# A hybrid decoder trunk on one core: scores read negated and scaled, an undivided first softmax, roots' rows by the values' bank, and a cast tied later

## The chip, the core and the metric

One core of one Trainium2 chip runs the whole program. Its engines are TensorE (PE; PEld is its weight load), VectorE (DVE), ScalarE (ACT), GpSimd (POOL) and SyncE (SP, which only issues transfers here). The metric is the device time of one execution in microseconds; the time of a kernel is the median of its runs.

## The reference

One layer works on 512 tokens of 1024 features. After a modulated RMS norm, one projection feeds two token mixers. Mixer A is a sliding-window attention (window 128, 8 query heads on 2 key heads, a sink for each head). Mixer B is a differential attention with 4 heads. Cut to what the change touches:

```python
# A: per head, with a sink as one more column of the softmax
bias = -slopes[:, :, None, None] * delta
scores = where(valid, scores + bias, -1e30)
probs = softmax(concatenate([scores, sink], -1), -1)[..., :-1]
# B: two maps per head, their difference, a norm over the head's 128 values
scores = scores - slopes * delta            # causal
p = softmax(scores, -1)
a = p[:, :, 0] - lam * p[:, :, 1]
out = einsum('bhqs,bshe->bqhe', a, v)
out = out * rsqrt(mean(out * out, -1) + 1e-6) * subln_g * (1 - lam_init)
```

Both mixers go through a branch projection and a sigmoid gate, are added, and go through an output projection (`merged @ w_out`); then follow a norm, a gated MLP of 2816 features with a short causal convolution, and a final norm.

## The kernel before

Every product runs in three passes: an operand is split into a high part (a cast on ScalarE, e.g. line 118) and a low part (a subtraction on VectorE), and `mm3` (lines 120 to 123) multiplies high by high, high by low and low by high. PSUM's eight banks are handed out under four names: f (2, for projections), s (3, scores), t (2, transposes) and v (1, values). An instruction that writes a bank waits until the bank's last tenant was read.

The order of TensorE's work is written by hand (`manual_schedule`). The projections are generators that give one `mm3` a step; `fill(n)` (line 519) takes n such steps ("ticks") between two pieces of an attention, so that TensorE has projections to multiply while the other engines do the softmax. `after(n, fn)` runs `fn` n ticks later. VectorE's and ScalarE's order in the attentions comes from priorities: what stands under `high_priority` is placed as soon as its operands can be there, and `issue_after` ties an instruction behind another. Each engine takes its own list in order.

Mixer A runs in four pairs of heads (j = 0, 1). `swa_scores` multiplies queries (`qa`) and keys into an s bank and one VectorE operation adds the distances and takes the greatest score (line 582); `swa_softmax` turns the greatest into the negated shift `nm` (593), has ScalarE take exponentials with their sums (597) and divides (605). The first pair begins while VectorE still empties the banks of the opening projections: `keep_v` (455) splits the values' banks `av0` to `av3` into `vvh` and `vvl`, and `stack` (431) makes `qa[:, 1]` for the second pair.

Mixer B runs in four heads of four blocks of queries (n = 0 to 3, with (n+1) x 128 keys). `diff_scores` and `diff_softmax` do the same for two maps; the two sums are inverted together, the second is multiplied by -lambda (`nlam`), the second map is scaled (704) and the first is scaled and added (705). `diff_transpose` turns the result on TensorE (`td`) and splits it into `aTh` and `aTl`; `diff_values` (720) multiplies it with the values into the v bank (`od`). Six ticks behind, `stats` sums squares on TensorE (`pss`, a t bank), a root follows on VectorE and GpSimd, `to_rows` (99) turns the root's column on TensorE (a t bank again), ScalarE copies it out (103), and two transfers spread it as a row `rb`; `spread` multiplies the head by `rb` and splits it (`vv`). `double` (443) makes the doubled keys `qk` of a head, the last two copies of 64 x 1024 on ScalarE (450).

Behind the mixers, `load_rows` loads the eight row blocks of the output weight (`wo`), each scaled by the first gate and split. `to_rows` also turns the second gate's column (`g2`, line 983), the last use of a t bank ahead of the output projection, whose eight accumulators (`oc`) take all eight banks. `prep(0, "m5", ...)` (1135) splits `m5w`, the sum of two blocks of the MLP's weight, which an accumulating transfer of GpSimd puts together (1076). Where these splits stand on ScalarE and VectorE follows from priorities and ties alone.

Of the kernel before, what the change touches and what calls it, by code (L numbers as in the profile page):

```python
# [8 lines left out]
F32 = mybir.dt.float32  # L9
# [22 lines left out]
G1_AT = 12  # L32
STAT_LAG = 6
ROW_LAG = 6
NORM_LAG = 20
# [11 lines left out]
def kernel(  # L47
# [45 lines left out]
    def vbank(name):  # L93
        return bank("v", 1, [P, S], name)
# [4 lines left out]
    def to_rows(dst, lo, n, name):  # L99
        turned = tbank(name, (P, P))  # L100
        nc.tensor.transpose(turned, cols[:, lo + n - P : lo + n], ident)
        part = cpool.tile([32, P], F32, tag="part", name=name + "p")
        nc.scalar.copy(part, turned[96:])
        d = dp.tile([n, P], F32, name=name + "d")
        nc.gpsimd.dma_start(d, part[32 - n :])
        nc.gpsimd.dma_start(dst, d.rearrange("k q -> (k q)").partition_broadcast(P))
# [336 lines left out]
    def double(dst, src):  # L443
        with tc.high_priority(offset=HP):
# [4 lines left out]
            for j, (own, other) in enumerate(halves):  # L449
                nc.scalar.copy(dst[other, j], dst[own, j])  # L450
# [109 lines left out]
    def swa_scores(i, n0):  # L560
        if n0 == 0:
            c = pairs[i] = Pair()
            c.mx, c.nm, c.lsum, c.es = (
                ap.tile([P, 2, NT], F32, tag=t, bufs=2, name=f"{t}{i}") for t in ("mx", "nm", "lsum", "es")
# [13 lines left out]
        for j in range(2):  # L578
            for n in (n0, n0 + 1):
                w = P if n == 0 else 2 * P  # L580
                with tc.high_priority(offset=HP):
                    c.last = nc.vector.tensor_tensor_reduce(
                        c.sb[n][:, j, :w], sps[j][:, n - n0, :w], dsw[:, 256 - w : 256], 1.0, -3e38, ALU.add, ALU.max,
                        c.mx[:, j, n : n + 1],
                    )

    def swa_softmax(i):
        with tc.high_priority(offset=HP):
            c = pairs[i]
            for j in range(2):  # L590
                h = i + 4 * j
                slope = 2.0 ** -(h + 1)
                nc.vector.tensor_scalar(c.nm[:, j], c.mx[:, j], -slope, nsink[:, h : h + 1], ALU.mult, ALU.min)
                nc.scalar.activation(c.es[:, j], c.nm[:, j], AF.Exp, bias=sink[:, h : h + 1])
                for n in range(NT):
                    w = P if n == 0 else 2 * P
                    nc.scalar.activation(
                        c.sb[n][:, j, :w], c.sb[n][:, j, :w], AF.Exp, bias=c.nm[:, j, n : n + 1], scale=slope,
# [64 lines left out]
    def diff_scores(*ss):  # L663
# [14 lines left out]
        for s, sps, w in ops:  # L678
# [3 lines left out]
            for m in range(2):  # L682
                st = ap.tile([P, w], F32, tag="st", bufs=ST, name=f"sd{h}_{n}_{m}")
                with tc.high_priority(offset=HP):
                    nc.vector.tensor_tensor_reduce(
                        st, sps[m], ddf[:, 512 - w : 512], 1.0, -3e38, ALU.add, ALU.max, mx[:, m : m + 1]
# [4 lines left out]
    def diff_softmax(s):  # L691
        with tc.high_priority(offset=HP):
            h, n = divmod(s, NT)
            slope = 2.0 ** (-2 * (h + 1))
            mx, pm = scored[s]
            lsum = ap.tile([P, 2], F32, tag="dls", bufs=3, name=f"dls{h}_{n}")
            nc.vector.tensor_scalar_mul(mx, mx, -slope)  # L697
            for m in range(2):
                nc.scalar.activation(  # L699
                    pm[m], pm[m], AF.Exp, bias=mx[:, m : m + 1], scale=slope, accum_out=lsum[:, m : m + 1]  # L700
                )
            nc.vector.reciprocal(lsum, lsum)
            nc.vector.tensor_mul(lsum[:, 1:2], lsum[:, 1:2], nlam)
            nc.vector.tensor_scalar_mul(pm[1], pm[1], lsum[:, 1:2])
            end = nc.vector.scalar_tensor_tensor(pm[0], pm[0], lsum[:, 0:1], pm[1], ALU.mult, ALU.add)
# [14 lines left out]
    def diff_values(h):  # L720
# [14 lines left out]
        def stats():  # L735
            pss = tbank(f"pss{h}", (P, NT))
# [3 lines left out]
            rstd_m2(rs, pss, NT, P, ap)  # L740
# [9 lines left out]

            after(ROW_LAG, lambda: to_rows(rb, NCOL + NT * h, NT, f"rs{h}"))
            after(NORM_LAG, spread)

# [51 lines left out]
    pairs, firsts, scored, probs, aTs = {}, {}, {}, {}, {}  # L805
# [12 lines left out]
    with tc.issue_after(pairs[0].last.ins), tc.issue_after(vat_copy.ins):  # L818
        with tc.high_priority(offset=HP):
            keep_v(6, (1,))  # L820
        swa_softmax(0)
        stack(qa[:, 1], acc[2], qsc[:, 1:2], soon=False, high=False)
        keep_v(4, (1,))
# [43 lines left out]
    for s in range(4 * DIFF_HEADS):  # L867
# [19 lines left out]
        if n == 0 and h:  # L887
            diff_values(h - 1)
            fill(DIFF_FILL[3])
# [143 lines left out]
    wo = []  # L1033
    for k in range(KT):
        with ExitStack() as place:
            for b in recent if k == 0 else merged[-2:] if k == 6 else ():
                place.enter_context(tc.issue_after(b.ins))
            wo.append(load_rows(wout, k, f"wo{k}", g1b))

# [95 lines left out]
    prep(0, "m5", (m5w[:, 0], m5w[:, 1]))  # L1135
# [711 lines left out]
```

## Time and profile before

| | |
|---|---|
| median of three runs | 680.46 us (680.43 to 682.62) |
| the profiled execution | 680.85 us, span 679.1 us |
| granted TensorE clock, mean | 0.998 |

Each row of a timeline gives a start, a duration, the engine, the line, the operation with output and inputs (partitions x elements), and in brackets how long the engine sat idle before it and what released it. "x2" stands for so many instructions in a row. TensorE's matmuls overlap: those of 128 x 512 last 0.39 us each and start every 0.227 us. A row of waits names who waited, for what, the total in us, how often, and the longest. Times in the text are from the start of the span.

### The profile page before, as it was taken

To read this page: it belongs to the slowest core of one execution; us is meant where nothing else is said; L and a number is where in the kernel's file an instruction comes from. 1 tells how busy PE (TensorE), PEld (TensorE's weight loads), DVE (VectorE), ACT (ScalarE), POOL (GpSimd) and SP (SyncE) were. 2 spreads that over 40 slices of the span, in tenths; PEclk is the share of its full clock that TensorE was granted. 3 is DMA by queue.
4 is the path that set the end of the run, shared out by engine and by line. 5 is a ranking of instruction groups with operands and counts; after the bars stand their busy time and mean duration, and the time that the engine had idled before them with its cause. 6 is when DMAs were issued, how large, how long until landed. Compare 5 with 4: busy or idle time off the path is not lost.

```text
span 679.1 us, 10811 instructions
## 1 busy us (share of the span) xinstructions
PE 666.5 (98%) x4021; PEld 591.7 (87%) x4021; DVE 569.8 (84%) x1055; ACT 402.6 (59%) x704; POOL 71.8 (11%) x86
## 2 busy tenths in 40 slices
PE   8999999999999999989999999999999999999995
PEld 8888888788888888868899999999999998888885
DVE  6988887779887678953689998888888999979997
ACT  6678879455655323232597656565556566656665
POOL 2000000000001000010020110011111003440300
PEclk9999999999999999999999999999999999999999
DMA  8961132444365698567374988887976658996903
GB/s 351 409 240 66 63 100 88 136 144 149 91 195 171 215 322 265 196 204 245 117 125 110 222 212 202 195 201 167 216 173 181 144 186 196 194 200 191 165 0 124
DMA packets 71876, 121.78 MB, mean 179 GB/s; under 512 B 4208, under 2 KB 48016, under 8 KB 71824
## 3 DMA queue, kind: packets, MB, share of 16 engines
q1 hardware_dynamic: 52960, 95.04, 41.6%
q0 software_dynamic: 18576, 25.71, 22.4%
q8 instruction: 31, 0.51, 0.3%
q10 hardware_dynamic: 288, 0.34, 0.2%
q14 instruction: 21, 0.17, 0.1%
HBM read 118.97 MB, written 2.11 MB: 178 GB/s over the span
## 4 chain that ended last, share of the span: by engine, by line
PE 82%; DVE 8%; DMA 5%; ACT 3%; issue 1%; POOL 0%; SPq 0%; ACTq 0%; POOLq 0%
PE up L1173 33%; PE dc L1776 15%; PE av L364 3%; DMA s_t<-in_w_up_dram 2%; PE oc L1229 2%; PE oc L1233 2%; PE oc L1230 2%; DMA wbd<-in_w_branch_diff_dram 2%; PE pga L121 2%; PE pga L122 2%; DVE ra L772 2%; PE aqa L361 2%; PE pga L123 2%; PE sw L577 1%; PE sd L674 1%
## 5 line engine op out<-in xcount | busy, mean ns | idle before, releaser
L1173 PE MATMUL up<-t,m_whi 128*128 128x256 f32 x512 | 93.1, 283 | 0.0
L1173 PEld LDWEIGHTS up<-t,m_whi 128*128 128x128 f32 x512 | 79.9, 192 | 0.0
L1173 PE MATMUL up<-t,m_wlo 128*128 128x256 f32 x256 | 72.4, 283 | 0.0
L1173 PE MATMUL up<-bh,p_whi 128*128 128x256 f32 x232 | 65.7, 283 | 0.0
L1173 PE MATMUL up<-bl,p_whi 128*128 128x256 f32 x232 | 65.7, 283 | 0.0
L1173 PE MATMUL up<-bh,p_wlo 128*128 128x256 f32 x232 | 65.7, 283 | 0.0
L1173 PEld LDWEIGHTS up<-t,m_wlo 128*128 128x128 f32 x256 | 49.2, 192 | 0.0
L1173 PEld LDWEIGHTS up<-bh,p_whi 128*128 128x128 f32 x232 | 44.5, 192 | 0.0
L1173 PEld LDWEIGHTS up<-bl,p_whi 128*128 128x128 f32 x232 | 44.5, 192 | 0.0
L1173 PEld LDWEIGHTS up<-bh,p_wlo 128*128 128x128 f32 x232 | 44.5, 192 | 0.0
L1076 POOL DMA_DIRECT2D s<-in_w_up_dram x21 | 27.0, 1366 | 157.5 <-DMA s<-in_w_up_dram 102.3
L1104 ACT CAST m_whi<-s 128x1024 fp32r<-128x1024 f32 x31 | 32.5, 1048 | 15.7 <-DVE s L1098 9.1
L772 DVE CUSTOM_DVE_ANT_0 ra<-ra,csb 128x1024 f32<-128x1024 f32 x32 | 38.6, 1219 | 2.8 <-DMA ra<-in_w_ada_t_dram 2.8
L1108 DVE TENSOR_TENSOR m_wlo<-s,m_whi 128x1024 fp32r<-128x1024 f32 x31 | 37.7, 1217 | 1.3 <-ACT m_whi L1104 1.3
L1173 PE MATMUL up<-t,p_whi 128*128 128x256 f32 x176 | 32.2, 283 | 0.0
L1173 PEld LDWEIGHTS up<-t,p_whi 128*128 128x128 f32 x176 | 27.4, 192 | 0.1
L699 ACT ACTIVATE sd<-sd,dmx 128x128 f32<-128x128 f32 (+3 forms) x32 | 17.8, 557 | 16.3 <-DVE dmx L697 12.1
L1104 ACT CAST p_whi<-wa 128x1024 fp32r<-128x1024 f32 x18 | 18.8, 1043 | 12.6 <-PE up L1173 5.4
L1180 ACT ACTIVATE gT<-a,cols 128x512 f32<-128x512 f32 x22 | 17.6, 813 | 13.4 <-DVE a L1215 13.0
L1108 DVE TENSOR_TENSOR p_wlo<-wa,p_whi 128x1024 fp32r<-128x1024 f32 x18 | 22.0, 1222 | 4.0 <-ACT p_whi L1104 3.3
L1173 PE MATMUL up<-t,p_wlo 128*128 128x256 f32 x88 | 24.9, 283 | 0.0
L1098 DVE TENSOR_TENSOR s<-s,wa 128x1024 f32<-128x1024 f32 x20 | 24.3, 1217 | 0.1
(547 smaller groups left out, 2034.6 us busy)
## 6 DMA issues: line engine op xcount, KB each, us to landing
ra<-in_w_ada_t_dram SPq DMA_DIRECT2D x32, 512.0 KB, 4.2
wa<-in_w_up_dram SPq DMA_DIRECT2D x22, 512.0 KB, 4.3
s<-in_w_up_dram SPq DMA_DIRECT2D x21, 512.0 KB, 4.6
s<-in_w_up_dram POOLq DMA_DIRECT2D x21, 512.0 KB, 6.9
adaw<-in_w_ada_t_dram SPq DMA_DIRECT2D x15, 512.0 KB, 10.2
a<-in_w_up_dram SPq DMA_DIRECT2D x11, 512.0 KB, 4.8
b<-in_w_down_dram SPq DMA_DIRECT2D x10, 512.0 KB, 4.2
w<-in_w_first_dram SPq DMA_DIRECT2D x8, 512.0 KB, 10.2
```

What stands on the lines that cost most here:

```text
L121: nc.tensor.matmul(o, lh, rh, start=start, stop=False)
L122: nc.tensor.matmul(o, lh, rl, start=False, stop=False)
L364: nc.tensor.matmul(acc[i], ht[:, t : t + P], wts[k][w][:, S:], start=start, stop=stop)
L699: nc.scalar.activation(pm[m], pm[m], AF.Exp, bias=mx[:, m : m + 1], scale=slope, accum_out=lsum[:, m : m + 1])
L772: nc.vector.tensor_tensor_reduce(r, r, csb, 1.0, 0.0, ALU.mult, ALU.add, late_mod[:, idx : idx + 1])
L1076: nc.gpsimd.dma_start(dst, upblock(*blk), accum_op=ALU.add)
L1098: nc.vector.tensor_add(src, src, R[J, "a11" if name == "m6" else "a12"])
L1104: nc.scalar.copy(W[J, name][0], R[J, SRC[name]])
L1108: nc.vector.tensor_sub(lo, R[J, SRC[name]], hi.bitcast(F32))
L1173: nc.tensor.matmul(o[u], w[:, k, cu], b[:, k], start=name in ("p1", "m5", "p2") and k == 0 and x == 0, stop=k == 3 and x == 2, skip_group_ ...
L1180: nc.scalar.activation(grow(j), av[J][:, u], AF.Identity, bias=cv[:, 66 + j : 67 + j], scale=cv[:, 44 + j : 45 + j])
L1776: nc.tensor.matmul((bank2[u] if o is None else o)[:, sl], a[:, q, cu], b[:, q, sl], start=first_mm and x == 0, stop=last_mm and x == 2, sk ...
```

## The change

- The score operation also multiplies by minus the slope and keeps the least instead of the greatest. In mixer A it starts from the negated sink (`nsink`), so its result is `nm` itself; the separate operations on `mx` (lines 593 and 697) are gone, and the exponential is taken with a scale of -1. Each exponential depends on its own column only.
- Mixer B's first map is no longer divided by its sum l0. Only l1 is inverted and multiplied by l0 and nlam, and one pass adds the second map, so scaled, to the first. The head comes out l0 times too great, which the norm takes back: its epsilon becomes EPS times l0 squared (`e0`, passed as `plus`). The sums of a head's four blocks now live in one tile.
- `double` does one of its two last copies on VectorE.
- `pss` and the turned roots and gates use the single v bank, ScalarE's copy of them has high priority, the lags behind `od` grow, and one of the ticks that followed `od` stands before it.
- `keep_v(4, (1,))` (the low part of `av1`) moves up to follow `keep_v(6, (1,))`.
- m5w's split is tied behind the cast and the low part of the fifth block of the output weight.

```diff
+M5_AT = 4
 STAT_LAG = 6
-ROW_LAG = 6
-NORM_LAG = 20
+ROW_LAG = (16, 16, 16, 10)
+NORM_LAG = (30, 30, 30, 24)
...
-    def vbank(name):
-        return bank("v", 1, [P, S], name)
+    def vbank(name, shape=(P, S)):
+        return bank("v", 1, list(shape), name)
 
     def raw_tile(shape, name):
         return wp.tile(shape, F32, tag="raw", bufs=4, name=name)
 
     def to_rows(dst, lo, n, name):
-        turned = tbank(name, (P, P))
+        turned = vbank(name, (P, P))
         nc.tensor.transpose(turned, cols[:, lo + n - P : lo + n], ident)
         part = cpool.tile([32, P], F32, tag="part", name=name + "p")
-        nc.scalar.copy(part, turned[96:])
+        with tc.high_priority(offset=HP):
+            nc.scalar.copy(part, turned[96:])
...
             for j, (own, other) in enumerate(halves):
-                nc.scalar.copy(dst[other, j], dst[own, j])
+                (nc.vector.tensor_copy, nc.scalar.copy)[j](dst[other, j], dst[own, j])
...
-            c.mx, c.nm, c.lsum, c.es = (
-                ap.tile([P, 2, NT], F32, tag=t, bufs=2, name=f"{t}{i}") for t in ("mx", "nm", "lsum", "es")
+            c.nm, c.lsum, c.es = (
+                ap.tile([P, 2, NT], F32, tag=t, bufs=2, name=f"{t}{i}") for t in ("nm", "lsum", "es")
...
                 with tc.high_priority(offset=HP):
+                    h = i + 4 * j
                     c.last = nc.vector.tensor_tensor_reduce(
-                        c.sb[n][:, j, :w], sps[j][:, n - n0, :w], dsw[:, 256 - w : 256], 1.0, -3e38, ALU.add, ALU.max,
-                        c.mx[:, j, n : n + 1],
+                        c.sb[n][:, j, :w], sps[j][:, n - n0, :w], dsw[:, 256 - w : 256], -(2.0 ** -(h + 1)),
+                        nsink[:, h : h + 1], ALU.add, ALU.min, c.nm[:, j, n : n + 1],
...
                 h = i + 4 * j
-                slope = 2.0 ** -(h + 1)
-                nc.vector.tensor_scalar(c.nm[:, j], c.mx[:, j], -slope, nsink[:, h : h + 1], ALU.mult, ALU.min)
                 nc.scalar.activation(c.es[:, j], c.nm[:, j], AF.Exp, bias=sink[:, h : h + 1])
                 for n in range(NT):
                     w = P if n == 0 else 2 * P
                     nc.scalar.activation(
-                        c.sb[n][:, j, :w], c.sb[n][:, j, :w], AF.Exp, bias=c.nm[:, j, n : n + 1], scale=slope,
+                        c.sb[n][:, j, :w], c.sb[n][:, j, :w], AF.Exp, bias=c.nm[:, j, n : n + 1], scale=-1.0,
                         accum_out=c.lsum[:, j, n : n + 1],
...
                     nc.vector.tensor_tensor_reduce(
-                        st, sps[m], ddf[:, 512 - w : 512], 1.0, -3e38, ALU.add, ALU.max, mx[:, m : m + 1]
+                        st, sps[m], ddf[:, 512 - w : 512], -(2.0 ** (-2 * (h + 1))), 3e38, ALU.add, ALU.min,
+                        mx[:, m : m + 1],
...
             h, n = divmod(s, NT)
-            slope = 2.0 ** (-2 * (h + 1))
             mx, pm = scored[s]
-            lsum = ap.tile([P, 2], F32, tag="dls", bufs=3, name=f"dls{h}_{n}")
-            nc.vector.tensor_scalar_mul(mx, mx, -slope)
+            if n == 0:
+                sums[h] = ap.tile([P, 2, NT], F32, tag="dls", bufs=2, name=f"dls{h}")
+            l0, l1 = (sums[h][:, m, n : n + 1] for m in range(2))
             for m in range(2):
                 nc.scalar.activation(
-                    pm[m], pm[m], AF.Exp, bias=mx[:, m : m + 1], scale=slope, accum_out=lsum[:, m : m + 1]
+                    pm[m], pm[m], AF.Exp, bias=mx[:, m : m + 1], scale=-1.0, accum_out=(l0, l1)[m]
                 )
-            nc.vector.reciprocal(lsum, lsum)
-            nc.vector.tensor_mul(lsum[:, 1:2], lsum[:, 1:2], nlam)
-            nc.vector.tensor_scalar_mul(pm[1], pm[1], lsum[:, 1:2])
-            end = nc.vector.scalar_tensor_tensor(pm[0], pm[0], lsum[:, 0:1], pm[1], ALU.mult, ALU.add)
+            nc.vector.reciprocal(l1, l1)
+            nc.vector.scalar_tensor_tensor(l1, l0, nlam, l1, ALU.mult, ALU.mult)
+            end = nc.vector.scalar_tensor_tensor(pm[0], pm[1], l1, pm[0], ALU.mult, ALU.add)
             probs[s] = pm[0]
...
         def stats():
-            pss = tbank(f"pss{h}", (P, NT))
+            pss = vbank(f"pss{h}", (P, NT))
             for n in range(NT):
                 nc.tensor.matmul(pss[:, n : n + 1], sq[:, n * P : (n + 1) * P], ones[:, 0:1], start=True, stop=True)
             rs = cols[:, NCOL + NT * h : NCOL + NT * h + NT]
-            rstd_m2(rs, pss, NT, P, ap)
+            l0, e0 = sums[h][:, 0], sums[h][:, 1]
+            nc.vector.scalar_tensor_tensor(e0, l0, EPS, l0, ALU.mult, ALU.mult)
+            with tc.high_priority(offset=HP):
+                rstd_m2(rs, pss, NT, P, ap, plus=e0)
...
-            after(ROW_LAG, lambda: to_rows(rb, NCOL + NT * h, NT, f"rs{h}"))
-            after(NORM_LAG, spread)
+            after(ROW_LAG[h], lambda: to_rows(rb, NCOL + NT * h, NT, f"rs{h}"))
+            after(NORM_LAG[h], spread)
...
+            keep_v(4, (1,))
         swa_softmax(0)
         stack(qa[:, 1], acc[2], qsc[:, 1:2], soon=False, high=False)
-        keep_v(4, (1,))
...
         if n == 0 and h:
+            fill(1)
             diff_values(h - 1)
-            fill(DIFF_FILL[3])
+            fill(DIFF_FILL[3] - 1)
...
     oacc = eight("oc")
-    wo = []
+    wo, marks = [], []
     for k in range(KT):
         with ExitStack() as place:
             for b in recent if k == 0 else merged[-2:] if k == 6 else ():
                 place.enter_context(tc.issue_after(b.ins))
             wo.append(load_rows(wout, k, f"wo{k}", g1b))
+            marks.append((casts[0], lows[0]))
...
-    prep(0, "m5", (m5w[:, 0], m5w[:, 1]))
+    with tc.issue_after(marks[M5_AT][0].ins), tc.issue_after(marks[M5_AT][1].ins):
+        prep(0, "m5", (m5w[:, 0], m5w[:, 1]))
```

TensorE and ScalarE lists keep their lengths but for small pieces (ScalarE 599 to 596 instructions), VectorE's goes from 1028 to 997. What moves, at three places.

VectorE behind the first pair's scores, before (line 462 is `keep_v`, 439 the low parts of `qa[:, 1]`, 601 the sum with the sink, `w_0` a weight of a later projection):

```order
L462 TENSOR_TENSOR vvl<-av_146,vvh 128x4x128
L593 TENSOR_SCALAR nm_633<-mx_632,nsink 128x4 x2
L439 TENSOR_SCALAR qa<-aqa_142,qsc,qa 64x512 x2
L462 TENSOR_TENSOR vvl<-av_144,vvh 128x4x128
L462 TENSOR_TENSOR vvl<-av_147,vvh 128x4x128
L601 TENSOR_TENSOR lsum_634<-lsum_634,es_635 128x4
L829 TENSOR_TENSOR lp<-lamv 128x128
L602 RECIPROCAL lsum_634<-lsum_634 128x4
L118 TENSOR_TENSOR w_0_l<-w_0_720,w_0_h 128x1024
```

and now:

```order
L464 TENSOR_TENSOR vvl<-av_146,vvh 128x4x128
L464 TENSOR_TENSOR vvl<-av_144,vvh 128x4x128
L602 TENSOR_TENSOR lsum_633<-lsum_633,es_634 128x4
L441 TENSOR_SCALAR qa<-aqa_142,qsc,qa 64x512
L603 RECIPROCAL lsum_633<-lsum_633 128x4
L602 TENSOR_TENSOR lsum_633<-lsum_633,es_634 128x4
L441 TENSOR_SCALAR qa<-aqa_142,qsc,qa 64x512
```

Both values' low parts stand first; the two low parts of `qa` no longer stand together, and the second is behind the sum of the second head's exponentials (the second `lsum`).

VectorE at the third head's first two blocks, behind their scores, before (`aTl` is the low part of the block turned before, `ta` a gated branch, `dls` the sums):

```order
L118 TENSOR_TENSOR w_3_l<-w_3_1697,w_3_h 128x1024
L423 TENSOR_TENSOR aTl_1540<-td_3_1742,aTh_1539 128x4x128
L702 RECIPROCAL dls_1_1757<-dls_1_1757 128x2
L703 TENSOR_TENSOR dls_0_1749<-dls_0_1749,nlam 128x1
L800 TENSOR_SCALAR ta<-ta,pA_1703 128x512
L703 TENSOR_TENSOR dls_1_1757<-dls_1_1757,nlam 128x1
L704 TENSOR_SCALAR sd_0_1_1720<-sd_0_1_1720,dls_0_1749 128x128
L704 TENSOR_SCALAR sd_1_1_1725<-sd_1_1_1725,dls_1_1757 128x256
L705 TENSOR_SCALAR sd_0_0_1718<-sd_0_0_1718,dls_0_1749,sd_0_1_1720 128x128
L705 TENSOR_SCALAR sd_1_0_1723<-sd_1_0_1723,dls_1_1757,sd_1_1_1725 128x256
```

and now (`ra` is a row product of the modulation):

```order
L120 TENSOR_TENSOR w_3_l<-w_3_1657,w_3_h 128x1024
L704 RECIPROCAL dls_1709<-dls_1709 128x1
L705 TENSOR_SCALAR dls_1709<-dls_1709,nlam 128x1 x2
L706 TENSOR_SCALAR sd_0_0_1678<-sd_0_1_1680,dls_1709,sd_0_0_1678 128x128
L706 TENSOR_SCALAR sd_1_0_1683<-sd_1_1_1685,dls_1709,sd_1_0_1683 128x256
L776 ISA ra_1720,late_mod<-ra_1720,csb 128x1024
L776 ISA late_mod 128x1
L425 TENSOR_TENSOR aTl_1512<-td_3_1702,aTh_1511 128x4x128
L804 TENSOR_SCALAR ta<-ta,pA_1663 128x512
```

The combining passes (706) stand ahead of `aTl` and `ta`, the scaling passes (704) are gone, and the row product that stood ahead of `w_3_l` has moved ahead of the scores.

ScalarE at the end of the merge, before (`mg3h` are the merged rows, 103 the copy of the turned gate):

```order
L118 COPY mg3h<-tdall 128x512
L118 COPY m5w<-s_t_2960 128x1024
L103 COPY g2p<-g_2869 32x128
L118 COPY mg3h<-tdall 128x512
L178 ACT_TABLE_LOAD
L178 ACTIVATE warm<-tdall 128x1
L118 COPY wo_h<-wo_2913 128x1024
L118 COPY wo_h<-wo_2920 128x1024
```

and now:

```order
L120 COPY mg3h<-tdall 128x512
L105 COPY g2p<-g_2817 32x128
L120 COPY mg3h<-tdall 128x512
L180 ACT_TABLE_LOAD
L180 ACTIVATE warm<-tdall 128x1
L120 COPY wo_h<-wo_2861 128x1024
L120 COPY wo_h<-wo_2868 128x1024
L120 COPY m5w<-s_t_2908 128x1024
L120 COPY wo_h<-wo_2875 128x1024
```

m5w's cast has gone from ahead of the gate's copy to behind two casts of the output weight.

More of the change, by code (lines that the diff above doesn't have):

```diff
@@ L803, in add_gate_a @@
         units.append((load, branch))
-    pairs, firsts, scored, probs, aTs = {}, {}, {}, {}, {}
+    pairs, firsts, scored, probs, aTs, sums = {}, {}, {}, {}, {}, {}
     ada = ada_rows()
```

## Prediction

> **What bounds the kernel now.** I read four views in turn: busy time on the page, TensorE's waits grouped by line, the busy time of short stretches, and the timeline of single engines where TensorE stood.
>
> ```profile
> PE 666.5 (98%) x4021; PEld 591.7 (87%) x4021; DVE 569.8 (84%) x1055; ACT 402.6 (59%) x704; POOL 71.8 (11%) x86
> ```
>
> TensorE (PE) is busy 98% of the span. The change leaves it as many matmuls of the same shapes, so it can only win what PE waits, and no other engine's saved time counts by itself. All of those waits, by the instruction that waited and what released it (total, times, longest):
>
> ```profile
> PE oc L1229 <- ACT g2p L103: 2.2, 1, 2.2
> PE td L715 <- DVE sd L705: 1.2, 2, 0.8
> PE ava L232 <- POOL ones L129: 1.1, 1, 1.1
> PE av L364 <- ACT hThA L350: 0.5, 1, 0.5
> PE pqa L121 <- DVE vvl L462: 0.3, 1, 0.3
> ```
>
> The third and fourth lie in the opening, which the change does not touch. The other three are 3.7 us in four places. Three stretches of 17 us that hold two of td's and the one of oc (PE, PEld, DVE, ACT and POOL busy, then the granted clock):
>
> ```profile
> 119.00:136.00 17.00, 16.21 (x79) 13.30 (x79) 13.12 (x37) 8.30 (x20) 0.00 (x0) 1.00 0.42 139
> 153.00:170.00 17.00, 16.61 (x85) 13.75 (x84) 16.18 (x46) 9.69 (x23) 1.32 (x2) 1.00 0.48 152
> 289.00:306.00 17.00, 14.79 (x66) 11.90 (x65) 9.86 (x11) 6.42 (x9) 1.89 (x2) 1.00 0.69 207
> ```
>
> What PE lacks to 17.00 is 0.79, 0.39 and 2.21 us; the wait of pqa is 0.33. Behind a wait the first matmul also starts its pipeline anew: the one at 301.85 below takes 0.50 where its neighbours take 0.39, and the next starts 0.34 after it instead of 0.23. So a wait costs its idle time and 0.1 to 0.2 more: 0.95, 0.55, 2.45 and, for pqa, 0.45. All four together are 4.4 us, 0.65% of the span. That is the ceiling.
>
> **The cast tied later.** Place four, ScalarE's timeline and then PE's (start, duration, instruction, and in brackets the idle time before it with its releaser):
>
> ```profile
> 293.74 0.62 ACT L118 CAST mg3h<-tdall 128x512 fp32r<-128x512 f32 x1 [2.85 <-DVE tdall L952]
> 300.47 1.04 ACT L118 CAST m5w<-s_t 128x1024 fp32r<-128x1024 f32 x1 [6.11 <-DMA s_t<-in_w_up_dram]
> 301.54 0.26 ACT L103 COPY g2p<-g 32x128 f32<-32x128 f32 x1
> ...
> 308.58 1.05 ACT L118 CAST wo_h<-wo 128x1024 fp32r<-128x1024 f32 x1 [3.81 <-PE oc L1233]
> ```
>
> ```profile
> 294.82 0.27 PE L101 MATMUL g<-ident,cols 128*128 128x128 f32 x1
> ...
> 301.85 0.50 PE L1229 MATMUL oc<-wo_h,mg0h 128*128 128x512 f32 x1 [2.21 <-ACT g2p L103]
> ```
>
> ScalarE takes its work in order. m5w's cast stands there 6.11 us for an accumulating transfer; behind it is g2p, the copy that empties the bank of the turned g2 column, and PE needs that bank. Now g2p follows mg3h directly: g is there at 295.09, so the copy ends near 295.4. The turned g2 also moves to the v bank, whose next user is the last of the eight accumulators, first written by the 15th matmul after g (294.84 and fourteen starts of 0.23, near 298.1). Margin 2.7 us; both reasons remove the wait independently. The bounds are 2.2 (bare idle) and 2.5; I take **-2.45**. The cast (1.04) and its VectorE subtraction (1.20, as another of that size below) now stand behind the fifth output weight. The cover is ScalarE's idle time there: 3.81 us before that cast, because PE has to release a weight buffer first. Without that cover 1.04 us would fall on the next weight.
>
> **Places two and three: the softmax of the differential heads.** PE turns the first block of a head (td) when VectorE has divided, scaled and combined it.
>
> ```profile
> 112.77 2.12 ACT L450 CAST qk<-qk 64x1024 fp32r<-64x1024 f32 x2
> ...
> 117.78 0.40 ACT L699 ACTIVATE sd<-sd,dmx 128x128 f32<-128x128 f32 x1
> ...
> 120.65 0.54 DVE L704 TENSOR_SCALAR sd<-sd,dls 128x128 f32<-128x128 f32 x2
> 121.11 0.73 DVE L705 SCALAR_TENSOR_TENSOR sd<-sd,dls,sd 128x128 f32<-128x128 f32 x2
> 121.60 0.30 PE L715 MATMUL td<-ident,sd 128*128 128x128 f32 x1 [0.79 <-DVE sd L705]
> ```
>
> One of the two qk casts of 1.06 leaves ScalarE, so its line up to the exponentials moves from 117.78 to 116.72. VectorE gets the copy instead. The trace has no such copy there: the one-source pass over 128x1024 nearest in kind took 0.75 (xn, line 1259), a two-source pass of that size 1.20 (w_l below). Nearest is 0.75, but I charge the margin 1.2; below nothing it cannot be, VectorE has to do it. With 1.2 the scores end some 1 us later than at 115.7, in time for exponentials at 116.7 to 116.8. Two low parts of 1.2 follow and end at 119.2. Behind them L704 (0.54 for two) is gone, the new three-operand pass is L705's kind on swapped operands: the first td block is ready at 120.2 to 120.3. PE wants it at 121.60-0.79 = 120.81. Margin 0.5: **-0.95**; at worst 0.
>
> ```profile
> 163.29 1.20 DVE L118 TENSOR_TENSOR w_l<-w,w_h 128x1024 fp32r<-128x1024 f32 x1
> 164.45 0.69 DVE L423 TENSOR_TENSOR aTl<-td,aTh 128x512 fp32r<-128x512 f32 x1
> ...
> 165.19 0.68 DVE L800 SCALAR_TENSOR_TENSOR ta<-ta,pA 128x512 f32<-128x512 f32 x1
> ...
> 165.85 0.54 DVE L704 TENSOR_SCALAR sd<-sd,dls 128x128 f32<-128x128 f32 x2
> 166.31 0.74 DVE L705 SCALAR_TENSOR_TENSOR sd<-sd,dls,sd 128x128 f32<-128x128 f32 x2
> ```
>
> Here VectorE is full (16.18 of 17). In the new order aTl and ta stand behind the combining pass and L704 is gone: 0.61+0.59+0.46 from start to start is 1.7 us, and L697 and the separate product with nlam are small change on top; the ready time falls by 1.7 at least, and PE, itself 0.95 earlier, waits for nothing. **-0.55**; at worst 0. What L704's other passes free on VectorE is worth nothing, since no wait of PE hangs on them. The new epsilon (one pass over 128x4 a head, 0.35 for two of that size in L593 below) stands behind pss, where nobody on PE waits.
>
> **Place one: the wait moves.** pqa needs the bank that vvl (av1) empties.
>
> ```profile
> 64.51 0.35 DVE L593 TENSOR_SCALAR nm<-mx,nsink 128x4 f32<-128x4 f32 x2
> 64.90 1.51 DVE L439 SCALAR_TENSOR_TENSOR qa<-aqa,qsc,qa 64x512 fp32r<-64x512 f32 x2
> 66.42 1.29 DVE L462 TENSOR_TENSOR vvl<-av,vvh 128x512 fp32r<-128x512 f32 x2
> ```
>
> ```profile
> 64.77 0.30 ACT L594 ACTIVATE es<-nm,sink 128x4 f32<-128x4 f32 x1 [1.50 <-DVE nm L593]
> ...
> 69.43 1.37 ACT L436 ACTIVATE qa<-pqa,qsc 64x512 fp32r<-64x512 f32 x2
> ```
>
> ```profile
> 67.97 1.08 PE L577 MATMUL sw<-ka,qa 128*128 128x128 f32 x8
> ```
>
> vvl now runs ahead of both qa low parts and is done near 65.2, so pqa starts near 66.7. But the second qa low part (half of 1.51, 0.76) now stands on VectorE behind the addition that needs the last exponential of this pair. The exponentials no longer wait for nm and can start 1.50 earlier; what ended at 69.5 (where ScalarE turns to the next qa) ends at 68.0, and near 67.4 since the copy of va, 0.5 to 0.6 of that stretch, now comes after them. With the addition and 0.76, qa is ready at 68.3, or 69.0 with the copy still between. The scores that read it come up on PE at 67.5 without the wait; the row's second kind started at 68.1 before. So a net **+0.2**, bounds -0.45 (all hidden) and +0.9.
>
> **Handoffs that come closer.** rs and pss move into the single v bank, rows turn and norms spread later. The last head's od now needs the bank that the copy of the third head's rs empties, three matmuls after its transpose; the last vvl is made later.
>
> ```profile
> 235.82 0.69 DVE L118 TENSOR_TENSOR vvl<-of,vvh 128x512 fp32r<-128x512 f32 x1
> ```
>
> It slips from 235.82 by the four ticks of the last lag (12 matmuls, 2.7 us) and by a row product or two of the modulation, 1.2 us each, that may now precede it, to 238.5 or 240.9; the merge wants it near 241 (242.6 in the trace by PE's place, less the 1.3 won by then, and a few tenths). Both handoffs at nothing; if one is late it costs its lateness, 0.4 to 1.6.
>
> Sum: -2.45-0.95-0.55+0.2 = -3.75. The profiled execution took 680.85, so 677.1; that execution lies 0.39 above the median of 680.46, so **676.7**.
>
> **Rivals.**
> - All four waits go: the chain for qa ends early enough. 680.46-4.4 = 676.1. For it: the exponentials start free. Against: the order on VectorE.
> - A wait reappears at one handoff (the td at 121.6, od of the last head, the last vvl, or qa at its upper bound): +0.4 to +3, so 677.1 to 679.5. For it: margins of 0.4 to 0.5, smaller than a single 1.2 us pass that falls differently. Against: PE went through the same stretches with all other handoffs in time.
> - The tie does not free ScalarE: m5w's cast still stands before the copy that PE needs, since its new place is behind a weight and not behind a time. Then -1.3 only: 679.2. Against: in the order g2p comes first, with five rows of ScalarE between.
> - Slower: one v bank for od, pss and rs. ScalarE's copy of rs is placed early on an engine that works in order; if the root's chain is late, everything behind waits, PE at od included.
>
> ```profile
>   PE rs L101: 3.2, 1
> ```
>
> So long ScalarE already stood before the third head's copy, waiting for rs on PE. If PE stood so before od at three heads, with the copy's 0.26 (as g2p), that is +10.4: 687.1. It decides from (3.75+3.4)/3 = 2.4 us a head. Against: the copies come a dozen matmuls ahead of od at the first two heads.
>
> The Trainium skill (TensorE: Matmul & The Clock Gate, Part 1: The HAM clock gate) says that PE's clock halves after an idle window of about 3.4 us and returns after as long a busy one. By that rule the slower rival's waits of 3.5 us could each cost an estimated 1.7 more, and 687.1 would become 692. In this trace the 2.21 us wait left the clock at 1.00, which agrees; no row has a wait long enough to test it.
>
> **How the numbers follow.** Forecast 0.46 (own range 676.1 to 677.1), all four gone 0.10, one handoff back 0.29, the tie without effect 0.03, slower 0.12. Within 0.5% of 680.46, about what a measurement of this kernel can tell from no change, means 677.06 to 683.86. Faster: 0.46+0.10 = 0.56; same: 0.29+0.03 = 0.32; slower 0.12. The range reaches from all four gone, less 0.3, to the worst single handoff: 675.8 to 680.0.
>
> **What would show it.** The wait for g2p gone and its copy near 295; both waits of td gone, none over 0.3 in their place; a wait of the scores for qa near 67.5 to 68.4 in the place of pqa's; m5w's cast near 306 to 310 with no wait of oc behind it. The forecast is wrong if oc still waits, if od or pB waits for a copy or a vvl by over 0.4, or if VectorE's copy of qk takes over 1.5.

## The result, and the profile after

The changed kernel takes 686.08 us (684.84 to 688.23, six runs), the kernel before 681.05 in the same series (680.27 to 682.62): 5.0 us more, ratio 1.0072, 95% interval 1.0051 to 1.0092. It is slower, outside the forecast's range (675.8 to 680.0) and on its other side.

The profiled execution took 685.63 (span 683.9 against 679.1). The page's first part, then TensorE's waits:

```profile
PE 668.9 (98%) x4021; PEld 592.5 (87%) x4021; DVE 567.4 (83%) x1023; ACT 397.4 (58%) x700; POOL 73.4 (11%) x86
```

```profile
PE pB L124 <- DVE vvl L120: 1.7, 1, 1.7
PE tp L617 <- ACT pT L619: 1.3, 2, 0.9
PE pga L123 <- ACT ta L787: 1.2, 1, 1.2
PE ava L234 <- POOL ones L131: 1.1, 1, 1.1
PE sw L579 <- DVE qa L441: 0.6, 1, 0.6
PE sd L675 <- DVE qk L452: 0.5, 1, 0.5
PE av L366 <- ACT hThA L352: 0.5, 1, 0.5
PE sd L675 <- DVE dmx L686: 0.3, 1, 0.3
PE aka L260 <- DVE cols L264: 0.2, 1, 0.2
PE td L716 <- DVE sd L706: 0.2, 1, 0.2
```

oc no longer waits for g2p, nor pqa for vvl, nor the two td blocks of before for sd; but pB, tp, pga, sw and sd are new in the list. VectorE has 2.4 us and ScalarE 5.2 us less to do: the work was saved and the time was not.

Where the 4.8 us arise is read by laying the same matmul of both traces side by side. Its start in the changed kernel less its start before, behind each place where that difference moves:

| matmul | before | changed | difference | what moved |
|---|---|---|---|---|
| pqa, second step | 67.17 | 66.74 | -0.43 | the wait for vvl goes |
| sw, second head of pair two | 68.14 | 68.48 | +0.33 | a wait for qa comes |
| tp of pair two | 85.71 | 86.98 | +1.27 | new wait for pT |
| tp of pair three | 98.06 | 99.81 | +1.75 | new wait for pT |
| td, head one | 121.60 | 122.45 | +0.86 | the wait for sd goes |
| td, head three | 166.80 | 167.20 | +0.40 | the wait for sd goes |
| sd, head four | 183.23 | 184.76 | +1.53 | new waits for qk and a bank |
| td, head four | 191.29 | 193.36 | +2.07 | new wait for sd |
| pga, behind its wait | 201.80 | 206.79 | +4.99 | new wait, and half clock |
| od, head four | 212.97 | 218.28 | +5.31 | short wait |
| pB, first block | 242.68 | 249.94 | +7.26 | new wait for vvl |
| oc | 301.85 | 306.87 | +5.02 | the wait for g2p goes |

Nothing moves behind that. The four terms of the forecast are all in the table, at +0.2 for place one (-0.57 and +0.79), -0.94, -0.55 and -2.38. The rest are new waits and the half clock behind one of them (about 1.7 us). The tie shows in this row of the changed kernel, where g2p follows the cast of mg3h at once:

```profile
302.73 0.26 ACT L105 COPY g2p<-g 32x128 f32<-32x128 f32 x1
```

**The product with rb.** VectorE, ScalarE and TensorE near 201, in order of time:

```profile
200.92 0.95 PE L739 MATMUL pss<-ones,sq 128*128 128x1 f32 x8
201.15 0.69 DVE L752 TENSOR_TENSOR of<-of,rb 128x512 f32<-128x512 f32 x1 [5.38 <-DMA rb<-rs1d]
201.87 0.62 ACT L120 CAST vvh<-of 128x512 fp32r<-128x512 f32 x1 [4.46 <-DVE of L752]
202.40 0.59 ACT L787 ACTIVATE ta<-pga 128x512 f32<-128x512 f32 x1
202.52 0.69 DVE L120 TENSOR_TENSOR vvl<-of,vvh 128x512 fp32r<-128x512 f32 x1 [0.68 <-ACT vvh L120]
202.89 1.04 ACT L120 CAST wga_h<-wga 128x1024 fp32r<-128x1024 f32 x1
203.04 0.56 PE L123 MATMUL pga<-hThA,wga_h 128*128 128x512 f32 x1 [1.17 <-ACT ta L787]
```

This reads from the bottom up: pga needs the bank that ta's tanh empties; the tanh stands behind the cast of vvh; the cast waits for the product with rb; and the product stood 5.38 us on VectorE for the transfer of rb. Its chain, from ScalarE's copy over GpSimd's queue:

```profile
191.32 0.26 ACT L105 COPY rs1p<-rs 32x128 f32<-32x128 f32 x1
191.87 0.58 POOL L107 DMA_DIRECT2D rs1d<-rs1p  x1 [13.61 <-ACT rs1p L105]
196.09 0.57 POOL L108 DMA_DIRECT2D rb<-rs1d  x1 [3.64 <-DMA rs1d<-rs1p]
```

The same head in the kernel before, where the product found rb there:

```profile
182.57 0.26 ACT L103 COPY rs1p<-rs 32x128 f32<-32x128 f32 x1
183.12 0.58 POOL L105 DMA_DIRECT2D rs1d<-rs1p  x1 [6.61 <-ACT rs1p L103]
186.94 0.57 POOL L106 DMA_DIRECT2D rb<-rs1d  x1 [3.23 <-DMA rs1d<-rs1p]
192.91 0.68 DVE L748 TENSOR_TENSOR of<-of,rb 128x512 f32<-128x512 f32 x1
```

From the end of the copy to the product were 10.1 us (182.83 to 192.91); in the changed kernel VectorE was at the product after 4.2 (191.58 to 195.77) and rb after 9.6. The same hold is on VectorE at the other heads of the changed kernel: 2.2, 6.7 and 3.8 us. The last is what pB waits for, since vvl stands four instructions behind the product:

```profile
245.17 0.69 DVE L752 TENSOR_TENSOR of<-of,rb 128x512 f32<-128x512 f32 x1 [3.75 <-DMA rb<-rs3d]
245.78 1.22 DVE L120 TENSOR_TENSOR wgd_l<-wgd,wgd_h 128x1024 fp32r<-128x1024 f32 x1
...
249.20 0.68 DVE L120 TENSOR_TENSOR vvl<-of,vvh 128x512 fp32r<-128x512 f32 x1
```

**The exponentials ahead of the copies.** ScalarE in pair two, then the turn that waits:

```profile
83.66 0.40 ACT L598 ACTIVATE st<-st,nm 128x128 f32<-128x128 f32 x1 [2.66 <-DVE nm L585]
83.97 0.19 ACT L598 ACTIVATION_READ_ACCUMULATOR st<-st,nm 128x1 f32 x1
84.06 1.04 ACT L120 CAST w_h<-w 128x1024 fp32r<-128x1024 f32 x1
85.12 1.20 ACT L438 ACTIVATE qk<-pq 64x512 fp32r<-64x512 f32 x2
86.34 0.97 ACT L619 COPY pT<-tp 128x512 f32<-128x512 f32 x2
```

```profile
86.98 0.98 PE L617 MATMUL tp<-ident,st 128*128 128x128 f32 x7 [0.95 <-ACT pT L619]
```

The exponential of one block now needs that block's scores alone, and so it is placed early: ScalarE stands 2.66 us for VectorE's score ahead of the cast of w, the two high parts of qk and the copies pT, which begin at 86.34. The kernel before had no exponential there:

```profile
85.07 0.97 ACT L618 COPY pT<-tp 128x512 f32<-128x512 f32 x2
```

### The profile page after: what moved, and what is told of

Its sections match the earlier page's. It is cut to its first block, busy times and chain, and to the rows that moved or that the text cites. A ratio compares the mean times of both kernels' runs of the same rounds, so it can differ in the third digit from the quotient of the medians.

```text
span 683.9 us, 10773 instructions
## 1 busy us (share of the span) xinstructions
PE 668.9 (98%) x4021; PEld 592.5 (87%) x4021; DVE 567.4 (83%) x1023; ACT 397.4 (58%) x700; POOL 73.4 (11%) x86
## 4 chain that ended last, share of the span: by engine, by line
PE 85%; DVE 6%; DMA 4%; ACT 3%; issue 2%; DVEq 0%; ACTq 0%; POOLq 0%
PE up L1180 32%; PE dc L1783 15%; PE av L366 3%; PE oc L1237 2%; PE oc L1240 2%; PE oc L1236 2%; PE aqa L363 2%; PE pgd L125 2%; PE pgd L123 2%; PE pgd L124 2%; PE pga L123 1%; PE pga L124 1%; PE pga L125 1%; DMA ra<-in_w_ada_t_dram 1%; PE sd L675 1%
```

## The experiments

Times are medians; a ratio is to the kernel before in the same series, with its 95% interval. That kernel's median was 681.05 us beside the changed kernel, 680.5 beside runs 1 to 8 and 681.96 beside runs 9 to 12; where runs of two series are compared below, it is by their medians.

**1. The old lags.**

```diff
-ROW_LAG = (16, 16, 16, 10)
-NORM_LAG = (30, 30, 30, 24)
+ROW_LAG = (6, 6, 6, 6)
+NORM_LAG = (20, 20, 20, 20)
```

> The changed kernel with the lags of before (rows turned 6 ticks behind the sums instead of 16 or 10, norms spread 20 instead of 30 or 24); everything else of the change stays, the single v bank too. Theory: the later rows make the transfers of rb land late, VectorE stands at the product with rb (5.4, 6.7 and 3.8 us in the changed kernel), and behind it the casts that free PE's banks and the last vvl come late. Then the wait of pga for ta (1.2), the half clock after it (1.7), the wait of pB for vvl (1.7 to 1.8) and od's 0.3 go: about 681.1, 4.9 us less than the changed kernel. Rival: the rows land late because transfers are slow at that time, whatever the lag, or the single v bank holds PE at the earlier place: 685 to 687.

Measured 678.71, ratio 0.9963 (0.995 to 0.9976). All waits of TensorE from 122 us on are gone, and only those of mixer A and of the opening are left:

```profile
PE tp L617 <- ACT pT L619: 1.3, 2, 1.0
PE ava L234 <- POOL ones L131: 1.1, 1, 1.1
PE aka L260 <- DVE cols L264: 0.8, 1, 0.8
PE sw L579 <- DVE qa L441: 0.6, 1, 0.6
PE av L366 <- ACT hThA L352: 0.5, 1, 0.5
```

That is 7.4 us by these two lines, against 4.9 expected: the waits of sd for qk and its bank at 184 and of td at 193 go with the lags too (VectorE stood 2.2 us at the first head's product, up to 173.9; that this hold made qk late is argued from the order). No wait for the single v bank is left, so with these lags it costs nothing.

**2. The exponentials tied behind the copies** of the pair before (all pairs but the first).

```diff
-        with tc.high_priority(offset=HP):
+        with tc.high_priority(offset=HP), tc.issue_after(pairs[i - 1].copy.ins) if i else ExitStack():
             c = pairs[i]
```

> The changed kernel with the exponentials of each later pair of mixer A tied behind ScalarE's copies of the pair before, the order that they had in the kernel before; nothing else is edited. Theory: without the operation that made nm, exponentials are placed ahead of the copies pT and stand there for their scores, so PE waits for a t bank twice (0.95 and 0.32 idle, 1.0 and 0.5 with the restart). Tied, both waits go: 684.6, 1.5 less. Rival: the copies are late because the score operations became slower (0.35 and 0.48 instead of 0.29 and 0.42): no more than 0.3 less.

Measured 683.82, ratio 1.0047 (1.0031 to 1.0064). Both waits of tp are gone: at the first td the same matmul stands 1.7 us earlier than in the changed kernel. Later, part is given back to a new wait of od for aTl (1.2). The time is 2.3 below the changed kernel, more than the 1.5 expected, and that is not all of tp's making: the profile has no half clock behind pga, which waits 0.87 here. Run 5 against run 1 gives the price without it.

**3. Both key copies on ScalarE again.**

```diff
-                (nc.vector.tensor_copy, nc.scalar.copy)[j](dst[other, j], dst[own, j])
+                nc.scalar.copy(dst[other, j], dst[own, j])
```

> The changed kernel with both last copies of the doubled keys on ScalarE again, as before. Theory: the copy on VectorE is what the scores of the last head wait for (0.50, and 0.32 for the bank behind it); it goes, 1.2 less with the restart. But the first td block (121.6 in the kernel before) was won by the same move: without it the wait of 0.95 comes back. Net 685.8, within 0.5 of the changed kernel, with the waits moved. Rival: td keeps its gain without the copy, since L704 alone made VectorE early enough: 684.9.

Measured 686.5, ratio 1.0083 (1.0064 to 1.0102): no difference in time, but not by the way that I expected. td keeps its gain at both heads (the rival was right there), sd's wait at 184 is gone, and a third turn of mixer A waits 1.85 us for pT, which now stands behind two casts of keys and the early exponentials.

**4. The tie alone**, in the kernel before.

```diff
-    prep(0, "m5", (m5w[:, 0], m5w[:, 1]))
+    with tc.issue_after(marks[4][0].ins), tc.issue_after(marks[4][1].ins):
+        prep(0, "m5", (m5w[:, 0], m5w[:, 1]))
```

> The kernel before with m5w's split tied behind the fifth output weight, and no other edit. Theory: this term is separate from all others, the wait of oc for g2p goes and nothing takes its place: 2.4 less than before, 678.7 by the median of 681.05. Rival: the turned g2 must leave the t bank too, or m5w's cast is late for something else: no more than 1 us less.

Measured 678.25, ratio 0.9958 (0.9942 to 0.9974). One line of order wins 2.3 us, and the v bank for g2 is not needed for it.

**5. Old lags and tied exponentials together.**

```diff
-ROW_LAG = (16, 16, 16, 10)
-NORM_LAG = (30, 30, 30, 24)
+ROW_LAG = (6, 6, 6, 6)
+NORM_LAG = (20, 20, 20, 20)
...
-        with tc.high_priority(offset=HP):
+        with tc.high_priority(offset=HP), tc.issue_after(pairs[i - 1].copy.ins) if i else ExitStack():
```

> The changed kernel with the lags of before and the exponentials tied behind the copies of the pair before. Theory: the lags and the exponentials placed early are independent losses, so both go: 678.7 (lags alone) less the 1.5 of the two waits of tp, 677.2, with only the wait of the scores for qa left of the new ones. Rival: the tie pushes exponentials late for the products that follow, as the wait of od for aTl (1.2) in the run with the tie alone suggests: 678.4.

Measured 677.29, ratio 0.9952 (0.9938 to 0.9966), as forecast (677.2): the two losses are independent, and the wait of sw for qa is the only new one left.

**6. And qa's low parts ahead of the sums**, on top of run 5.

```diff
             keep_v(4, (1,))
+        stack(qa[:, 1], acc[2], qsc[:, 1:2], high=False)
         swa_softmax(0)
-        stack(qa[:, 1], acc[2], qsc[:, 1:2], soon=False, high=False)
```

> As the run with old lags and tied exponentials, and with both low parts of qa placed on VectorE ahead of the sums of the first pair. Theory: the wait of the scores for qa (0.63, 0.8 with its restart) goes too, qa being ready near 66.7 when the scores come at 67.5: 676.4, with no wait of PE left behind the opening. Rival: the divisions of the first pair come later by the second sum, and the first turn of pair one waits in its place: 677.0 to 677.5.

Measured 676.62, ratio 0.9947 (0.9933 to 0.9961). The wait for qa is gone, and no turn waits in its place; by the medians, 0.7 us more was to be had at place one. The profiled execution, the slowest of the five (677.81; the others 676.28 to 677.24), has a wait of od instead:

```profile
PE od L124 <- DVE aTl L425: 0.9, 1, 0.9
```

**7. The new lags alone**, in the kernel before.

```diff
-ROW_LAG = 6
-NORM_LAG = 20
+ROW_LAG = (16, 16, 16, 10)
+NORM_LAG = (30, 30, 30, 24)
...
-            after(ROW_LAG, lambda: to_rows(rb, NCOL + NT * h, NT, f"rs{h}"))
-            after(NORM_LAG, spread)
+            after(ROW_LAG[h], lambda: to_rows(rb, NCOL + NT * h, NT, f"rs{h}"))
+            after(NORM_LAG[h], spread)
```

> The kernel before with the new lags only (t banks, no other edit). Theory: the lags alone make rb land late and hold VectorE at the product with rb, as in the changed kernel: waits of PE for a cast or copy behind it near 183 to 205 (1 to 3 us with a half clock) and for the last vvl (1.8): 683.5 to 686. Rival: the lags harm only with VectorE's other work moved too (the copy of the keys, the first softmax): 680 to 681.

Measured 690.3, ratio 1.0152 (1.0132 to 1.0173), worse than either theory. TensorE's waits:

```profile
PE td L715 <- DVE sd L705: 5.1, 4, 2.2
PE oc L1229 <- ACT g2p L103: 3.0, 1, 3.0
PE pB L122 <- DVE vvl L118: 1.6, 1, 1.6
```

VectorE stood 7.1 and 6.6 us at products with rb, and behind the first of them two td blocks waited 1.9 and 2.2 us; the other two waits of td are those of before. The profiled execution is again the slowest (692.86; the others 690.13 to 690.44), with half clock behind two of its waits. So the lags alone do the harm, 9.8 us by the medians, and the rest of the change softened it.

**8. Rows early, norms late**, in the changed kernel.

```diff
-ROW_LAG = (16, 16, 16, 10)
+ROW_LAG = (6, 6, 6, 6)
```

> The changed kernel with the rows turned 6 ticks behind the sums as before, and the norms still spread at the new, later ticks. Theory: what hurts is the time from the turn of the root to the product with rb, over which two transfers run; with 24 (head four: 18) ticks between them instead of 14, rb has landed and VectorE is not held: about 678.7, as with both lags old. Rival: the later product itself is the harm (the last vvl comes 4 ticks, 2.7 us, later than in the kernel before, and pB waits for it): 680 to 682.

Measured 679.53, ratio 0.9985 (0.9977 to 0.9994). In this run no instruction on VectorE waits for rb at all. What the turn of the rows cost is thereby told apart from the later product: with 24 ticks between them (18 at the last head) instead of 14 the hold is gone, which is 6.6 us less than the changed kernel. The later product costs the remaining 0.8 against run 1 (td of the last head waits 0.4).

**9. One more tick ahead of the last od**, on top of run 6.

```diff
-    fill(4)
+    fill(5)
     diff_values(DIFF_HEADS - 1)
```

> As the run with old lags, tied exponentials and early qa, and with one more tick of projections ahead of the last head's od. Theory: that run's profile has one wait left behind the opening, od for aTl (0.9, 1.05 with its restart); three matmuls of 0.23 more in front cover 0.7 of it: about 675.8. Rival: VectorE stands there for something that follows PE (the bank of td, a cast), and aTl comes later by as much: 676.6.

Measured 676.61, ratio 0.9933 (0.9917 to 0.9949). The profile has only the waits of the opening:

```profile
PE ava L234 <- POOL ones L131: 1.1, 1, 1.1
PE av L366 <- ACT hThA L352: 0.5, 1, 0.5
```

The wait of od is gone from the profile, but the median is that of run 6, and the 675.8 expected was missed. The wait may have stood in the slower executions of run 6 alone; only one of them was profiled. This version beats both kernels, the changed one by 9.5 us and the one before by 0.67% in a series where that one was slow (run 6, with the same median, by 0.53%), and in its profile TensorE waits for nothing from 15 us on.

**10. The sums of squares two ticks earlier**, in the changed kernel.

```diff
-STAT_LAG = 6
-ROW_LAG = (16, 16, 16, 10)
-NORM_LAG = (30, 30, 30, 24)
+STAT_LAG = 4
+ROW_LAG = (18, 18, 18, 12)
+NORM_LAG = (32, 32, 32, 26)
```

> The changed kernel with the sums of squares (pss) two ticks earlier, and rows and norms as many ticks later behind them, so that they stay where they were. In the changed kernel PE's clock was at half for 3.4 us (203.3 to 206.7) behind the wait of pga (1.17), right before which stand eight matmuls of one column each (0.95 us with hardly any work in the array). Theory: short stretch without work, 1.2 to 2.1 us, is enough to lose the clock where it falls badly, and pss ahead of the wait lengthens it; moved away, the wait stays near 1.2 and the half clock goes, at least in most runs: 684.4, 1.7 less. Rival: the wait alone does it: no change, 686.

Measured 685.54, ratio 1.0059 (1.004 to 1.0079). In the profile pga waits even longer, with no half clock behind it (the section on the hardware). In time the run settles nothing, since sd now waits 2.0 for qk and od 1.1 for aTl.

**11. Both key copies on ScalarE**, on top of run 6.

```diff
-                (nc.vector.tensor_copy, nc.scalar.copy)[j](dst[other, j], dst[own, j])
+                nc.scalar.copy(dst[other, j], dst[own, j])
```

> As the run with old lags, tied exponentials and early qa, but both last copies of the doubled keys on ScalarE as before. Theory: ScalarE then has the kernel before's order around the turns, where no turn waited, and td's gain does not need the copy (the run with the copy on ScalarE kept it): 676.6, no difference. Rival: ScalarE needs the relief, td of the first head (0.95) or a turn of a later pair (up to 2) waits again: 677.5 to 678.6.

Measured 678.26, ratio 0.9956 (0.994 to 0.9973): 1.6 more than run 6, and than run 9 of the same series.

```profile
PE td L716 <- DVE sd L706: 1.3, 2, 0.9
```

These are the td blocks of heads three (0.94, at 165.96) and four. The first head's does not wait. The copy on VectorE is worth 1.6 us once the rest is clean, which run 3 could not show.

**12. The scaled scores and the undivided softmax of mixer B alone**, in the kernel before (`diff_scores` and `diff_softmax` as in the change).

```diff
-            rstd_m2(rs, pss, NT, P, ap)
+            l0, e0 = sums[h][:, 0], sums[h][:, 1]
+            nc.vector.scalar_tensor_tensor(e0, l0, EPS, l0, ALU.mult, ALU.mult)
+            rstd_m2(rs, pss, NT, P, ap, plus=e0)
```

> The kernel before with mixer B's scores negated and scaled and its first softmax undivided (its sum in the norm's epsilon), and no other edit. Theory: the two waits of td for sd (0.95 and 0.55 with restart) go by this part alone, since L704 and the separate scaling leave VectorE: 1.5 less than the kernel before, 679.0. Rival: the first of them needs ScalarE's relief by the copy, the second the new order: 680 to 680.6.

Measured 683.33, ratio 1.0033 (1.0015 to 1.0052), slower. Both waits of td are gone, as expected (-0.95 and -0.55 at 121.60 and 166.80). But:

```profile
PE oc L1231 <- ACT g2p L103: 3.2, 1, 3.2
PE rs L101 <- DVE cols L164: 3.1, 1, 3.1
```

The steps of the root, which have no high priority here, fell behind a row product, low parts and scores on VectorE (its last step ran at 181.25, the sums were read at 175.13), and PE stood 3.1 us for its turn at the old lag of 6. In the changed kernel the root has that priority, and run 1 has the old lag without this wait, so there the longer lags were not needed. That the priority is what does it is argued; no run takes it alone away.

## Why the prediction was wrong

- **The sum's four terms held.** The tie: forecast -2.45, measured -2.38, and alone -2.3 (run 4); g2p ends at 302.99, which less the 7.4 us that had been lost by then is 295.6, where 295.4 was forecast. The two td blocks: -0.95 and -0.55, measured -0.94 and -0.55; run 12 shows that the softmax part alone brings both, so the move of a keys' copy off ScalarE, from which the prediction worked out the first, was not needed for it; and run 11 shows that the second hangs on the keys' copy too when the rest is clean. Place one: forecast +0.2, measured +0.22, by the mechanism that I gave (sw stands 0.63 us for qa). Sum -3.65 against -3.75.
- **The step that failed is "Handoffs that come closer", where both were put "at nothing"**, and what it left out. I named od and the last vvl, with the slip of vvl counted in ticks of PE and row products. What decided was the time of two dependent transfers between the turn of the root and the product with rb. The fence in that step showed vvl, and not the product ahead of it on VectorE. The turn moved by the same ticks as the product, so I took their distance as kept. But the code ties the product behind the low parts of the last two weights on VectorE, not to PE, and VectorE came to it earlier than PE's ticks say: 4.2 us behind the copy of rs at the second head, when rb needed 9.6 (from 191.58 to 201.15). Runs 1, 7 and 8 show it from three sides: 7.4 us of the changed kernel hang on the two lags, 6.6 of them on the time between turn and product (run 8) and 0.8 on the later product itself. The step gave a late vvl a price of 0.4 to 1.6; pB alone lost 2.0 (it waits 1.7, and the prediction had named a wait there of over 0.4 as a sign of being wrong), and sd, td and pga, which the step did not name, lost the rest, with the half clock behind pga.
- **Missing altogether: ScalarE's order in mixer A.** I counted the removal of `nm` as work saved, and at place one as a free start of the exponentials. The operation also held the exponentials back behind the copies that PE's turns need. Its price is 1.5 us in the profile (+1.00 and +0.48), and 1.4 between runs 1 and 5, which differ in the tie alone.
- **The slower rival** was right in kind, an engine that works in order and stands for the root's chain, and wrong in place. In run 1 nobody waits for the v bank; it was VectorE at the far end of the transfers and not ScalarE at the copy. Its price of 3.5 us at three heads has no counterpart. That the time moved up, as this rival said, is no support for it. (The rival of one handoff that comes back adds up to 679.7 at its upper end, not 679.5; nothing hangs on it.)
- **Half clock**: the profile has one such stretch of 3.4 us at 1.17 us of wait. The Trainium skill (TensorE: Matmul & The Clock Gate, Part 1: The HAM clock gate) puts the idle window at about 3.4 us. The length of the half stretch agrees, its onset here does not: 1.17 us of idle time stood ahead of it. The measurement decides, and the prediction should have priced shorter waits too.

## What to carry to other kernels

An operation that is removed may have been what held its followers back on an engine that works in order: read from the new order what is now placed early, and what it stands in front of. When a transfer is moved together with its reader, compare the reader's place on its own engine with the transfer's landing in us, not in steps of another engine. Parts of a change that each win may be hidden by one that loses: here the new lags cost 7.4 us, and the same kernel with the old ones (run 1) is 1.8 us faster than the one before.

## What the runs showed of the hardware

The clock fell to half behind a short wait. In the changed kernel (columns: busy times of PE, PEld, DVE, ACT and POOL with counts, granted clock, DMA share, GB/s):

```profile
202.00:203.00 1.00, 0.00 (x0) 0.00 (x0) 0.48 (x1) 1.00 (x3) 0.00 (x0) 1.00 0.00 0
203.00:204.00 1.00, 0.96 (x3) 0.80 (x4) 1.00 (x4) 1.00 (x2) 0.00 (x0) 0.67 0.00 0
204.00:205.00 1.00, 1.00 (x5) 0.80 (x4) 1.00 (x3) 1.00 (x4) 0.00 (x0) 0.50 0.00 0
205.00:206.00 1.00, 1.00 (x4) 0.71 (x4) 0.96 (x5) 0.39 (x3) 0.20 (x1) 0.50 0.00 0
206.00:207.00 1.00, 1.00 (x4) 0.81 (x3) 0.29 (x1) 0.00 (x0) 1.00 (x1) 0.62 0.65 147
207.00:208.00 1.00, 1.00 (x6) 0.79 (x5) 0.78 (x2) 0.00 (x0) 0.19 (x1) 1.00 0.89 352
```

About 3.4 us at half, 1.7 us lost, behind 1.17 us of idle time and 0.95 us of matmuls with one column each. In run 10, where those matmuls stand elsewhere, 1.58 us of idle time left the clock at 1.00, and so did 0.87 with them ahead in run 2; in the kernel before 2.21 us did, and in run 12 a wait of 3.1 did while one of 3.2 did not. So the length of the wait does not decide alone.

The moment does too, as the traces show when they are laid side by side. Every half-clock stretch begins a whole multiple of 3.413 us behind the trace's first clock record and behind the others of its trace (in run 7 they begin at 214.50, 313.49 and 688.95, which are 29 and 110 times that apart), so the clock changes at the borders of a fixed grid. What counts is how much of one grid stretch TensorE spends in matmuls wider than one column (the ends of matmuls are modelled):

| run | grid stretch | in wider matmuls, us of 3.41 | clock in the next |
|---|---|---|---|
| 7 | 310.07 to 313.49 | 1.23 | half |
| 7 | 211.09 to 214.50 | 1.24 | half |
| 12 | 302.53 to 305.95 | 1.36 | half |
| 3 | 200.57 to 203.99 | 1.42 | half |
| changed | 199.93 to 203.34 | 1.45 | half |
| 12 | 179.65 to 183.07 | 1.51 | full |
| 10 | 181.95 to 185.36 | 1.51 | full |
| 2 | 198.75 to 202.17 | 1.76 | full |
| 10 | 202.43 to 205.84 | 1.83 | full |
| before | 300.26 to 303.68 | 1.83 | full |

From the first clock record on (4 to 7 us into the span), every stretch of the fourteen traces with 1.45 us or less was followed by half clock and every one with 1.51 or more by full clock. A wait across a border is shared out: the 3.1 us of run 12 fall as 1.16 and 1.90 on two stretches and left the clock full, the 2.2 of before as 0.62 and 1.59. The one-column matmuls count as idle time or nearly so: with them the changed kernel's stretch was busy for 2.24 us and still lost the clock.

The kernel before scatters over 3 us (679.5 to 682.7 in the first series of experiments), and mostly in two clusters, near 680 at a mean clock of 0.997 to 0.998 and near 682 at 0.995 to 0.996. With its wait of 2.2 us at oc gone, run 4 keeps within 0.2 us (678.16 to 678.35). That fits a half clock that this wait brings on where it falls into one grid stretch, as in the profile of run 7 behind its oc: one half stretch costs 1.7 us and takes 0.0025 off the mean clock (an estimate, 3.41/2 over 680). None of the upper cluster was profiled, so it stays an inference.

A score operation that starts its least from a column took 0.35 and 0.48 us (128 and 256 wide), and one that starts from a constant 0.29 and 0.42 on the same engine, in both kernels: 0.06 for the column. VectorE's copy of 64 x 1024 took 0.69, ScalarE's 1.04.
